# Sums of weights in HBM spread over the projections, with additions two behind their copies

## The chip, the cores and the metric

One core of a Trainium2 chip runs the kernel. The metric is device time in microseconds for one execution, lower being better. Times are medians over several executions, and profiles are of one execution each, which has its own time. A core has five engines that work side by side: TensorE (matmuls and transposes; PE in the profile), VectorE (DVE), ScalarE (ACT), GpSimd (POOL) and SyncE (SP, which here only issues transfers). Each goes through its own instructions in a fixed order, and waits on semaphores for the others. Transfers between HBM and the core's memory are issued by an engine into a queue, and 16 DMA engines carry them.

## The reference, cut to what matters

A decoder layer on 512 tokens of width 1024, all in float32:

```
h = rms_norm(x, norm_mix)
u, q, kc, vc, ks, vs, kw, vw, g_nsa, g_merge = split(h @ w_in)
y_pool = pool_mixer(u)                       # causal means over 2, 4, 8, 16 tokens, minus u, then w_pool
y_nsa  = nsa_mixer(q, ...)                   # 16 heads: compressed, selected and window attention, gated
g_a, g_b = split(sigmoid(g_merge))
x = x + (g_a * (y_pool @ w_proj_pool) + g_b * (y_nsa @ w_proj_nsa)) @ w_out
h = rms_norm(x, norm_mlp)
x = x + square(relu(h @ w_ff1)) @ w_ff2      # 1024 -> 4096 -> 1024
out = rms_norm(x, norm_final)
```

The compressed branch pools keys and values over 31 overlapping blocks of 32 tokens through a small MLP. At 512 tokens the selected branch takes all 8 blocks, so it and the window branch are causal attention, each over keys of its own.

## The kernel before, in words

**Arithmetic.** Each float32 operand is split into a high part of a shorter type (fp32r) and the remainder, its low part; a product is three matmuls: high by high, high by low, low by high (`mms`, L370). Activations stay on the chip. Weights come from HBM in pieces of 128 partitions by up to 1024 floats, 512 KB. ScalarE copies a piece into its high part (`wh`), and VectorE or POOL subtracts to get the low part (`wl`). For the projections, w_proj_nsa and w_out this goes by halves (L325 to L329): while attention and w_out run (`mode["pool"]`), VectorE makes the low part of the first half and POOL that of the second.

**Sums of weights.** Most of the MLP goes through seven block products in place of eight, in 14 groups (four column blocks of w_ff1 and three of w_ff2, two groups each). A group needs three sums of quarters of its weights, S1, S3 and S2, each 512 KB. They are formed in HBM long before the MLP loads them: a **copy**, which moves one quarter into the sum's place and is issued by SP (L256), then an **addition**, a DMA that adds a second quarter to what lies there and is issued by POOL (L252). S2 starts from a copy of the finished S1 (so its operands read S<-S in the profile). That makes 42 sums, in the list `jobs`: S1 and S3 of group 100, S1 and S3 of 101, S2 of 100, S1 and S3 of 200, S2 of 101 and so on (layer, block, group). Each addition waits on POOL for its copy to land, and each S<-S copy on SP for the addition of its S1. POOL computes nothing while it waits.

**Loads.** The list `LD` gives every piece of weights in order, 0 to 34 the projections of the first phase (`P1`: keys, values, compression MLP, pool branch, gates, first queries), 35 to 47 `FILL2` (queries q3 to q7 and gates gb0 to gb7), 48 to 55 w_proj_nsa (pn0 to pn7), 56 to 63 w_out (wo00 to wo13, half and row block), then from 64 (`MLP0`) the MLP. There are four raw buffers, so load i is issued when the piece i - 4 has been split. `emit_load` issues load i on SP (L223) and then calls `make_sum` as often as `sums_after(i)` says (L229 to L233). One call issues the addition of the sum before, on POOL, and the copy of the next sum, on SP; the compiler is told to keep the copy behind that load (`tc.issue_after`).

By `sums_after`, loads 0 to 36 start no sum, loads 37 to 51 start two each, then every second load to 62 starts one, and in the MLP every fourth.

**The stages, in the time of the profile.** Until about 44 us: norm and turning of the input. To 160: the projections of P1. Then FILL2, whose matmuls are there to fill TensorE beside the start of attention. Attention's first step (`cmp_scores`, L896 to L931): scores against compressed keys, a softmax on VectorE and ScalarE, the gate r (L916), and then on POOL the weighting `cw` (L918) and the split into `PC` (L920, L921). TensorE transposes PC into psT (L929), and nothing of the main loop is emitted ahead of that for the first pair of heads. The main loop runs over 96 slots (eight pairs of heads, query tiles, branches): scores (L959), maximum (L981), exponential (L991), weighting by the sum and the gate on POOL (L1004), transposes (L1020), their split (L1031 on ScalarE, L1035 on VectorE) and product with the values (L1045, L1054). It ends near 412. Then w_proj_nsa (pn), merging (L833), and w_out in two halves: the weights wo00 to wo03 are used as they come, four matmul groups of about 1.4 us each (psB L370), and wo10 to wo13 are split into a resident pair W1H, W1L, used once all four are there. The MLP starts near 480.

The order of the instructions is that in which the kernel's generator emits them: `ahead` (L344) puts a half of a weight's split between matmuls, a finished second half emits the next load, and the load emits its sums at that point. So a change of `sums_after` moves SP's copies and POOL's additions between other instructions.

Of the kernel before, what the change touches and what calls it, by code (L numbers as in the profile page):

```python
# [62 lines left out]
def trunk(ctx: ExitStack, tc: tile.TileContext, A, out):  # L63
# [41 lines left out]
    def add_key(k):  # L105
# [14 lines left out]
        else:  # L120
# [4 lines left out]
    P1 = ("ck ks u0 wk0 wk1 u1 wk2 u2 kw wk3 cv V0 V1 V2 wv0 u3 wv1 q0 wv2 wpool ga0 ga1 wv3 ga2 q1 "  # L125
          "ga3 ga4 ga5 q2 ga6 ga7 pp0 pp1 pp2 pp3").split()
    FILL2 = "gb0 q3 q4 q5 gb1 gb2 q6 gb3 q7 gb4 gb5 gb6 gb7".split()
# [7 lines left out]
    MLP0 = len(LD)  # L135
# [5 lines left out]
    jobs, late = [], []  # L141
# [62 lines left out]
    def emit_load():  # L204

        i = st["load"]
        if i >= len(LD):
            return False
        segs = LD[i]
        a = segs[0][0].shape[1]  # L210
        b = sum(s.shape[2] for s, _ in segs)
        assert a * b <= 1024
        if not by_name() or st["kept"] < RAW:
            st["kept"] += by_name()
            t = wp.tile([128, 1024], F32, tag="raw", bufs=RAW, name=f"raw{i}")
        elif spare:
            t = spare.pop(0)
        else:
            return False
        st["load"] += 1  # L220
        v = t[:, :a * b].rearrange("p (a b) -> p a b", a=a)
        for s, o in segs:
            began = nc.sync.dma_start(v[:, :, o:o + s.shape[2]], s)  # L223
        raws[i] = (t, a, b)
        for _ in range(sums_after(i)):
            make_sum(began)
        return True

    def sums_after(i):  # L229

        i -= len(P1) + 2
        n = len(FILL2) + 2
        return 2 if 0 <= i < n else i % 2 if n <= i < MLP0 - len(P1) - 2 else i % 4 == 0 and i > 0  # L233

    def by_name():

        return st["load"] >= MLP0

    def give_back(*tiles):
        spare.extend(tiles)  # L240
        while spare and by_name() and emit_load():
            pass

    def make_sum(load):

        n = st["sums"]
        if n > len(jobs):
            return
        st["sums"] += 1
        if n:  # L250
            to, _, q = jobs[n - 1]
            POOL.dma_start(to, q, accum_op=ALU.add)  # L252
        if n < len(jobs):
            to, q, _ = jobs[n]
            with tc.issue_after(load.ins):
                nc.sync.dma_start(to, q)  # L256
# [15 lines left out]
    def group_steps(i):  # L272

        key, at = WL[i]
        if isinstance(at, str):
            t = held.pop(key)
        else:
            while st["load"] <= at:
                assert emit_load()
            t = raws.pop(at)[0]  # L280
        h, l = slot_of(i)
        ACT.activation(h, t, AF.Copy)  # L282
        yield
        DVE.tensor_tensor(l, t, h.bitcast(F32), op=ALU.subtract)  # L284
        hls[i] = tuple(x.rearrange("p (a b) -> p a b", a=4) for x in (h, l))
        to = SUM_OF.get(key)
        if to is None:
            give_back(t)
        elif to not in held:
            held[to] = t  # L290
        else:
            yield
            DVE.tensor_tensor(t, t, held[to], op=ALU.add)
            give_back(held[to])
            held[to] = t

    def emit_prep_half():
# [12 lines left out]
        if "h" not in part:  # L310
            while st["load"] <= at:
                assert emit_load()
            if WL[i][0] in dest:
                h, l = dest[WL[i][0]][:2]
            else:
                h, l = slot_of(i)
            part.update(h=h, l=l, half=0)
# [295 lines left out]
    with ExitStack() as c1:  # L613
# [185 lines left out]
        for k in P1[2:]:  # L799
            i = int(k[-1]) if k[-1].isdigit() else None  # L800
# [35 lines left out]
    with ExitStack() as c2:  # L836
# [235 lines left out]
        n = len(slots)  # L1072
# [4 lines left out]
        for i in range(n + LAG + PLAG):  # L1077
            if i < n:
                p = slots[i][0]
# [480 lines left out]
```

## Time and profile before

| | |
|---|---|
| three runs | 841.06, 839.63, 840.54 us; median 840.54 |
| the profiled execution's own time | 837.06 us |
| its span in the profile | 835.1 us |
| mean granted clock of TensorE | 0.982 |

The profile has a page and views of the trace. In a row of instructions, L252 is line 252 of the kernel, `out<-in` are the names of its tiles, xN the number of instructions; in the view in order of time the first number is the start in us from the span's start, the second the length, and brackets hold the idle time of the engine just before and what ended it. In the table by windows each row gives the stretch, its length, the busy time of PE, PEld (weight loads into TensorE), DVE, ACT and POOL with their instructions, TensorE's granted clock as a share of full speed, the mean busy share of the 16 DMA engines (a little over 1 where the records overlap) and GB/s. A row of waits gives the engine, the tile and line that waited, what it waited for, total us, times, and the longest. In the table of DMA issues the last number is the median us from issue to landing. q1 is the queue of SP's transfers, q0 that of POOL's.

### The profile page before, as it was taken

The numbers are of one execution on the slowest core, as the hardware profiler recorded it, in microseconds if no ns is written. First come the engines' busy times: TensorE is split into PE (matmuls) and PEld (weight loads), VectorE is DVE, ScalarE is ACT, GpSimd is POOL, SyncE is SP. The second block draws the span as 40 slices with busy tenths as digits, with TensorE's granted clock in tenths as the row PEclk, the third lists the DMA queues.
The fourth block names the chain that finished last, engine by engine and source line by source line (L and its number), as shares of the span: only waits on it lengthen the run. The fifth ranks groups of instructions, "written<-read, shape, count | busy, mean of one in ns | idle before, by whom it ended". The sixth has DMA issues, their size and how long they took to land.

```text
span 835.1 us, 13944 instructions
## 1 busy us (share of the span) xinstructions
PE 792.6 (95%) x5081; PEld 708.6 (85%) x5081; DVE 614.2 (74%) x1195; ACT 483.8 (58%) x959; POOL 214.1 (26%) x277
## 2 busy tenths in 40 slices
PE   7999999983899899999999999999999999999997
PEld 4889878872787788888788789999999999999986
DVE  7796744531897998989766569897789678987823
ACT  6576533332686888789823457664575467446811
POOL 6000000024877797876233400100000000000000
PEclk9999999995899999999999999999999999999999
DMA  9364633599809988577397932968543644365402
GB/s 301 99 181 116 170 89 106 152 255 252 165 15 240 227 164 165 127 181 148 132 248 178 301 74 79 265 191 249 172 143 113 216 147 170 105 200 177 151 1 101
DMA packets 125502, 137.15 MB, mean 164 GB/s; under 512 B 5365, under 2 KB 112409, under 8 KB 125210
## 3 DMA queue, kind: packets, MB, share of 16 engines
q1 hardware_dynamic: 102970, 113.46, 42.6%
q0 software_dynamic: 22176, 22.02, 17.9%
q8 instruction: 40, 0.66, 0.3%
q10 hardware_dynamic: 288, 0.79, 0.3%
q14 instruction: 28, 0.23, 0.1%
HBM read 131.53 MB, written 46.14 MB: 213 GB/s over the span
## 4 chain that ended last, share of the span: by engine, by line
PE 63%; DVE 16%; DMA 7%; ACT 6%; issue 4%; POOL 2%; SPq 1%; ACTq 0%; POOLq 0%; DVEq 0%
PE psF L370 16%; PE psB L1329 13%; PE psB L370 12%; PE psB L1445 9%; DMA S<-w_ff 4%; PE psO L1054 2%; PE psT L1020 2%; PE psS L959 2%; DVE wl L284 2%; PE psV L370 2%; DVE PT L1035 1%; DVE P L981 1%; ACT P L991 1%; PE psF L424 1%; DMA raw<-w_out 1%
## 5 line engine op out<-in xcount | busy, mean ns | idle before, releaser
L370 PE MATMUL psF<-R,wh 128*128 128x512 f32 x512 | 166.8, 404 | 0.2 <-ACT MA L817 0.2
L282 ACT ACTIVATE wh<-raw 128x1024 fp32r<-128x1024 f32 x66 | 69.7, 1057 | 78.2 <-PE psB L1445 30.7
L327 ACT ACTIVATE wh<-raw 128x512 fp32r<-128x512 f32 (+1 forms) x102 | 61.3, 620 | 84.5 <-PE psF L370 35.8
L370 PEld LDWEIGHTS psF<-R,wh 128*128 128x128 f32 x512 | 92.6, 189 | 18.0 <-ACT MA L817 0.5
L1004 POOL TENSOR_SCALAR P<-P,sm,GT 128x128 f32<-128x128 f32 (+3 forms) x128 | 98.1, 979 | 21.5 <-DVE sm L1001 14.7
L370 PE MATMUL psF<-R,wl 128*128 128x512 f32 x256 | 101.8, 398 | 0.7 <-DVE wl L329 0.7
L252 POOL DMA_DIRECT2D S<-w_ff x42 | 53.9, 1283 | 177.9 <-DMA S<-w_ff 117.7
L284 DVE TENSOR_TENSOR wl<-raw,wh 128x1024 fp32r<-128x1024 f32 x66 | 80.4, 1220 | 22.3 <-ACT wh L282 22.1
L329 DVE TENSOR_TENSOR wl<-raw,wh 128x512 fp32r<-128x512 f32 (+1 forms) x78 | 56.1, 731 | 38.0 <-ACT wh L327 37.6
L991 ACT ACTIVATE P<-P,sm 128x128 f32<-128x128 f32 (+3 forms) x128 | 71.1, 557 | 18.2 <-DVE sm L981 16.7
L981 DVE CUSTOM_DVE_ANT_0 P<-psS,cst 128x128 f32<-128x128 f32 (+3 forms) x128 | 59.6, 483 | 23.6 <-PE psS L959 16.0
L1329 PE MATMUL psB<-R,wh 128*128 128x256 f32 x352 | 64.1, 282 | 0.0
L1525 POOL TENSOR_TENSOR MA<-x,GB 128x512 f32<-128x512 f32 x1 | 1.3, 1292 | 238.8 <-DVE sq L1205 238.8
L1031 ACT ACTIVATE PT<-psT 128x512 fp32r<-128x512 f32 (+2 forms) x96 | 49.2, 521 | 18.3 <-PE psT L1020 17.5
L1035 DVE TENSOR_TENSOR PT<-psT,PT 128x512 fp32r<-128x512 f32 (+2 forms) x96 | 56.6, 593 | 4.4 <-ACT PT L1031 3.5
L370 PEld LDWEIGHTS psF<-R,wl 128*128 128x128 f32 x256 | 48.3, 189 | 11.8 <-DVE wl L329 0.9
L282 ACT ACTIVATE w3h<-raw 128x1024 fp32r<-128x1024 f32 x32 | 33.8, 1057 | 39.6 <-PE psB L1445 14.8
L1020 PE MATMUL psT<-ident,P 128*128 128x128 f32 x320 | 52.1, 279 | 4.0 <-POOL P L1004 3.6
L1329 PEld LDWEIGHTS psB<-R,wh 128*128 128x128 f32 x352 | 54.1, 189 | 0.3 <-DVE R L1271 0.2
L1020 PEld LDWEIGHTS psT<-ident,P 128*128 128x128 f32 x320 | 40.4, 143 | 15.1 <-POOL P L1004 6.5
L329 POOL TENSOR_TENSOR wl<-raw,wh 128x512 fp32r<-128x512 f32 x28 | 41.5, 1483 | 37.0 <-ACT wh L327 37.0
L1329 PE MATMUL psB<-R,wl 128*128 128x256 f32 x176 | 49.4, 281 | 0.0
(431 smaller groups left out, 2319.1 us busy)
## 6 DMA issues: line engine op xcount, KB each, us to landing
raw<-w_ff SPq DMA_DIRECT2D x50, 512.0 KB, 4.1
S<-w_ff POOLq DMA_DIRECT2D x42, 512.0 KB, 7.5
raw<-S SPq DMA_DIRECT2D x42, 512.0 KB, 4.1
raw<-w_in SPq DMA_DIRECT2D x32, 512.0 KB, 4.1
S<-w_ff SPq DMA_DIRECT2D x28, 512.0 KB, 6.3
S<-S SPq DMA_DIRECT2D x14, 512.0 KB, 7.2
raw<-w_proj_nsa SPq DMA_DIRECT2D x8, 512.0 KB, 4.0
raw<-w_out SPq DMA_DIRECT2D x8, 512.0 KB, 5.1
```

The source lines that it names most:

```text
L282: ACT.activation(h, t, AF.Copy)
L284: DVE.tensor_tensor(l, t, h.bitcast(F32), op=ALU.subtract)
L327: ACT.activation(h[:, sl], t[:, sl], AF.Copy)
L329: eng.tensor_tensor(l[:, sl], t[:, sl], h[:, sl].bitcast(F32), op=ALU.subtract)
L370: PE.matmul(ps, a, b, start=first and j == 0, stop=last and j == n - 1, skip_group_check=True)
L981: DVE.tensor_tensor_reduce(out=P[:, o:o + n].rearrange("p (a c) -> p a c", c=128), in0=s, in1=m, scale=1.0, scalar=3e38, op0=ALU.add, op1= ...
L991: last_exp[:] = [ACT.activation(c, c, AF.Exp, bias=sm[:, 0, e:e + 1], scale=-1.0, accum_out=sm[:, 1, e:e + 1])]
L1004: POOL.tensor_scalar(P[:, o:o + n], P[:, o:o + n], sm[:, 2, e:e + 1], GT[:, qb, c + e:c + e + 1], op0=ALU.mult, op1=ALU.mult)
L1020: PE.transpose(pt[:, 128 * j:128 * j + 128], P[:, 128 * j:128 * j + 128], ident)
L1035: DVE.tensor_tensor(dL, src, dH.bitcast(F32), op=ALU.subtract)
L1329: PE.matmul(out, w[u][:, k, 128 * f:128 * f + 128], XB[x][v][:, k, :], **kw)
L1445: PE.matmul(out, YB[y][u][:, k, 128 * f:128 * f + 128], w[v][:, k, :], **kw)
```

## The change

Two things. `sums_after` is rewritten: of the P1 loads, 11, 13, ... 29 start one sum each (ten), loads 30 to 36 none, loads 37 to 51 one each instead of two, loads 52 to 63 in turn one, two and none, and in the MLP every fourth load, as before, but from load 64 where it was 65. And `make_sum` issues the addition of the sum two before, not of the one before, so that another copy lies between a copy and its addition.

```diff
@@ -222,15 +222,18 @@
         for s, o in segs:
             began = nc.sync.dma_start(v[:, :, o:o + s.shape[2]], s)
         raws[i] = (t, a, b)
-        for _ in range(sums_after(i)):
+        for _ in range(int(sums_after(i))):
             make_sum(began)
         return True
 
     def sums_after(i):
 
-        i -= len(P1) + 2
-        n = len(FILL2) + 2
-        return 2 if 0 <= i < n else i % 2 if n <= i < MLP0 - len(P1) - 2 else i % 4 == 0 and i > 0
+        p, f = len(P1), len(P1) + len(FILL2)
+        if i < p:
+            return 10 <= i < 30 and i % 2
+        if i < MLP0:
+            return p + 2 <= i < f + 4 or i >= f and i % 3
+        return i % 4 == 0
 
     def by_name():
 
@@ -244,11 +247,11 @@
     def make_sum(load):
 
         n = st["sums"]
-        if n > len(jobs):
+        if n > len(jobs) + 1:
             return
         st["sums"] += 1
-        if n:
-            to, _, q = jobs[n - 1]
+        if n > 1:
+            to, _, q = jobs[n - 2]
             POOL.dma_start(to, q, accum_op=ALU.add)
         if n < len(jobs):
             to, q, _ = jobs[n]
```

The lines behind are numbered three higher in the changed kernel.

## The prediction, made before the changed kernel ran

> **What bounds the kernel now.** I read the totals and the DMA queues, then the waits of TensorE, then busy time by window where TensorE falls short.
>
> ```profile
> PE 792.6 (95%) x5081; PEld 708.6 (85%) x5081; DVE 614.2 (74%) x1195; ACT 483.8 (58%) x959; POOL 214.1 (26%) x277
> ...
> q1 hardware_dynamic: 102970, 113.46, 42.6%
> q0 software_dynamic: 22176, 22.02, 17.9%
> ```
> ```profile
> PE psT L929 <- POOL PC L921: 14.7, 1, 14.7
> ```
> ```profile
> 80.00:100.00 20.00, 20.00 (x96) 16.43 (x95) 14.01 (x28) 8.96 (x17) 0.00 (x0) 1.00 0.75 199
> ...
> 180.00:200.00 20.00, 5.34 (x24) 3.99 (x22) 1.39 (x2) 2.25 (x5) 7.62 (x8) 0.69 1.14 247
> 200.00:220.00 20.00, 16.20 (x69) 13.53 (x69) 13.71 (x42) 10.11 (x31) 12.12 (x18) 0.71 1.04 249
> ...
> 460.00:480.00 20.00, 19.88 (x86) 15.81 (x85) 11.10 (x11) 8.55 (x15) 8.68 (x7) 1.00 0.98 304
> ```
> TensorE is busy for 95% of the span, so time can only come from where it is not. One wait of 14.7 us, behind POOL's PC at L921, is a third of all its idle time. It lies in 180 to 200, where TensorE works 5.34 of 20 us, its granted clock falls to 0.69, and the DMA engines are full (share 1.14, the last column but one). One addition costs 17.9% of 835.1 us over 42, 3.56 us of all 16 engines; a copy or a load of 512 KB costs q1's 42.6% over 113.46 MB, 1.64 us. Windows 80 and 460 are the stages that receive work: TensorE is full in both, the DMA at 0.75 and 0.98.
>
> The wait in POOL's and the other engines' order of time:
>
> ```profile
> 165.48 2.57 POOL L252 DMA_DIRECT2D S<-w_ff  x2 [35.12 <-DMA S<-w_ff]
> ...
> 174.27 1.36 POOL L329 TENSOR_TENSOR wl<-raw,wh 128x512 fp32r<-128x512 f32 x1 [0.61 <-ACT wh L327]
> ...
> 194.47 1.16 POOL L252 DMA_DIRECT2D S<-w_ff  x1 [5.11 <-DMA S<-w_ff]
> 195.11 1.15 POOL L918 TENSOR_TENSOR cw<-cw,c 128x256 f32<-128x256 f32 x1
> 195.85 1.55 POOL L252 DMA_DIRECT2D S<-w_ff  x1
> ...
> 197.76 1.30 POOL L920 TENSOR_SCALAR PC<-cw 128x256 fp32r<-128x256 f32 x1
> 199.14 0.72 POOL L921 TENSOR_TENSOR PC<-cw,PC 128x256 fp32r<-128x256 f32 x1
> ...
> 207.40 1.17 POOL L252 DMA_DIRECT2D S<-w_ff  x1 [4.22 <-DMA S<-w_ff]
> 208.15 2.15 POOL L1004 TENSOR_SCALAR P<-P,sm,GT 128x128 f32<-128x128 f32 x4
> ```
> ```profile
> 179.72 0.17 DVE L916 TENSOR_TENSOR c<-c,GT 128x8 f32<-128x8 f32 x1
> ```
> ```profile
> 199.92 0.75 PE L929 MATMUL psT<-identR,PC 128*128 128x128 f32 x4 [14.66 <-POOL PC L921]
> ...
> 209.12 0.89 PE L1020 MATMUL psT<-ident,P 128*128 128x128 f32 x2 [2.30 <-POOL P L1004]
> ```
> L918 could start when L916 is done at 179.9, but POOL goes in order and seven additions stand ahead of it, an eighth behind it, each waiting for its copy to land. TensorE is out of work at 199.92 - 14.66 = 185.26. A second wait follows at once: the softmax weights stand behind one more addition (207.40).
>
> **The change, part by part.** No arithmetic is added or removed: 42 copies and 42 additions stay, at other places. The built order puts ten additions before POOL's VC copies of L724 and four, not seven, ahead of L918, none between L918 and L921.
>
> ```profile
> raw<-w_in SPq DMA_DIRECT2D x4, 512.0 KB, 3.7
> ...
> S<-w_ff SPq DMA_DIRECT2D x2, 512.0 KB, 5.9
> ```
> ```profile
> S<-w_ff SPq DMA_DIRECT2D x5, 512.0 KB, 6.9
> S<-w_ff POOLq DMA_DIRECT2D x4, 512.0 KB, 12.1
> raw<-w_in SPq DMA_DIRECT2D x3, 512.0 KB, 12.9
> S<-S SPq DMA_DIRECT2D x1, 512.0 KB, 9.5
> ```
> ```profile
> 175.77 0.66 SPq L223 DMA_DIRECT2D raw<-w_in  x1
> ...
> 198.71 0.37 SPq L223 DMA_DIRECT2D raw<-w_in  x1
> 199.14 2.07 SPq L256 DMA_DIRECT2D S<-w_ff  x2
> ```
> These are issues with their median time to landing, first from 120 to 160 us, then from 160 to 180, then SP's order.
>
> *Ten sums moved into the projections* (from about 44 to 120 us): 10 x (3.56 + 1.64) = 52 us of DMA over some 75 us, beside a load of 0.75 in the window shown. Loads there may go from 3.7 towards 12.9 us. POOL is idle there (0.00), so the additions hold no engine; two behind, they find their copies landed. TensorE is covered by four raw buffers. I take 0; if the cover is gone, a load 9.2 us late costs at most that once.
>
> *The wait at L921.* The last of the four additions before L918 is that of S2 of group 201. Its copy (S<-S) is issued behind the load of gb2, 175.77 + 0.4 = 176.2. It lands 4.7 us later when alone (row below) and 9.5 us later among four additions; two are in flight now, so I take 7.4: 183.6. POOL then needs 0.2 to see it, 0.64 (195.11 - 194.47), and 0.74 + 1.38 + 0.78 from L918 to L929 without the pieces between: 3.7. L929 starts at 187.3, 12.6 earlier; the bounds are 14.66 (TensorE ready first) and 10.5.
>
> *The second wait stays.* After L921 come a low half (1.3 us), the load of q6 that it frees, the copy 0.43 behind (199.14 - 198.71) and its addition, still ahead of the first weights: 187.3 + 1.3 + 0.1 + 0.43 = 189.1, landing 5.9 to 8.3 later (207.40 - 199.14); I take 6.3, then 0.75: weights at 196.1, not 208.15. So 12.0 us are gained there, not 12.6: TensorE waits longer at L1020, and the low clock after it (0.71) stays.
>
> *Attention.* Fourteen additions leave POOL's line: 14 x 1.16 = 16 us of an engine off the path.
>
> ```profile
> 215.00:412.00 197.00, 188.49 (x1202) 163.48 (x1201) 170.91 (x546) 163.94 (x430) 143.59 (x191) 1.00 0.69 151
> ```
> TensorE is idle 8.5 us there; that bounds the gain, 0 the other way. I take 1.
>
> *The stage of w_out pays.* Loads 52 to 63, pn4 to wo13, start twelve sums, not six: 6 x 5.2 = 31 us of DMA more where it was near full. Three additions now stand ahead of the low half of pn6, two ahead of that of wo01.
>
> ```profile
> raw<-w_out SPq DMA_DIRECT2D x5, 512.0 KB, 5.6
> ...
> S<-S SPq DMA_DIRECT2D x1, 512.0 KB, 4.7
> ```
> ```profile
> 426.03 0.56 SPq L256 DMA_DIRECT2D S<-w_ff  x1
> ```
> ```profile
> 432.79 1.16 POOL L252 DMA_DIRECT2D S<-w_ff  x1 [1.62 <-DMA S<-w_ff]
> 435.44 1.33 POOL L329 TENSOR_TENSOR wl<-raw,wh 128x512 fp32r<-128x512 f32 x1 [1.49 <-ACT wh L327]
> ...
> 446.64 1.33 POOL L329 TENSOR_TENSOR wl<-raw,wh 128x512 fp32r<-128x512 f32 x1 [2.51 <-ACT wh L327]
> ...
> 454.31 1.80 POOL L329 TENSOR_TENSOR wl<-raw,wh 128x512 fp32r<-128x512 f32 x1
> ```
> ```profile
> 451.84 0.63 ACT L327 ACTIVATE W1H<-raw 128x512 fp32r<-128x512 f32 x1 [2.65 <-DMA raw<-w_out]
> 452.38 1.14 ACT L327 ACTIVATE wh<-raw 128x512 fp32r<-128x512 f32 x2
> ```
> ```profile
> 456.54 0.40 PE L370 MATMUL psB<-wh,mH 128*128 128x512 f32 x1
> ```
> In times of before: the third copy is issued at 427.4 and lands 6.9 to 12.9 later, I take 439; pn6's low half moves from 435.44 to 439.9, and the load that it frees with it. TensorE does not wait: it needs that half at 442.5 (two weights of 5.6 us before 450.94, less half of one). The next copy lands near 449, so wo00's low half runs at 449.8, not 446.64, and wo10's load is issued 3 us late, at 451.1. It lands 8 us later (between 5.6 and 12.9, two copies ahead of it), at 459.1, not 451.8. ScalarE takes wo10 first and wo01 (452.38) behind it, and wo01 is due at 456.54 with some 2.4 us to spare: TensorE waits 7.3 - 2.4 = 4.9. The new order also puts half of wo11 ahead of wo02 on ScalarE; wo11's load starts when wo01's low half is done, lands 5.6 later and needs 2 us of conversion, against 5.6 us of matmuls: 2 more. Together 7; the bounds are 0 (loads stay within the 2.4) and 16 (all at 12.9).
>
> The rows say 3.7 against 12.9 us for a load beside additions, though they are on another queue. The Trainium skill, DMA: Bandwidth & Descriptors, section on queues, rings and completion order, says that an engine takes turns between queues packet by packet. By that a w_out load, in 256 rows of 2 KB, lets fewer pieces of an addition pass than a w_in load in 1024 rows of 512 B; the second rival is what that would give.
>
> **Sum.** 0 - 12 - 1 + 7 = -6 us. The profiled execution's own time is 837.06 us (span 835.1): 831.1. The runs' median, 840.54, is 3.5 above it: 834.5.
>
> **Rivals.**
> Second, *the w_out loads hold*: they land in 5.6 us, as five of them do above, only 2 us later than alone, within the 2.4 to spare. Then -12 - 1 + 1 = -12, and 828.5. For it: w_out's rows are large, and the copies alone take 5.9. Against: wo10's load starts late whatever it takes.
> Third, *the w_out stage takes all back*, at wo01. If the third copy takes 12.9 us, pn6's low half and each load behind it starts 6 us late, and wo10's load lands 18 late in all (6 + 12.9 - 3.8 + 3): less 2.4, and 2 at wo02, 17.6 us against 13. That gives 845, slower. It decides from wo10 landing 13 us late. For it: 460 to 480 is at 0.98 before six more sums. Against: the largest delays stand beside four additions at once.
> Fourth, *the change misses its wait*: gb2's load and the copy behind it are as slow as now (12.9), L929 at 193, a gain of 7, all given back: 840.5.
>
> **Chances.** The forecast 0.44, the second 0.26, the third 0.17, the fourth 0.13. About 0.2% (1.7 us) can be told from no change. Faster: 0.44 + 0.26 + 0.03 of the fourth; same: 0.08 of it; slower: the third and 0.02. The forecast's own range is 830 to 838.5; with the second down to 826 and the third up to 843, less than 2 in 10 is left out.
>
> **What would show it.** Right: the wait at L929 under 4 us, one at L1020 of 4 to 6, weights near 196; new waits of TensorE for wl at the second and third w_out weights, ScalarE waiting for DMA raw<-w_out before W1H; the DMA share near 1 from 420 to 480. The forecast is wrong if POOL still waits for S ahead of L918 after 185 us, if TensorE waits in 44 to 160, or if no wait stands between 440 and 475.

## The result, and the profile after

The changed kernel is slower by 0.6%: median 845.41 us over 19 runs (840.73 to 852.67) against 841.06 us (836.76 to 843.86) for the kernel before, a ratio of 1.006 with a 95% interval of 1.0037 to 1.0082. The forecast was 834.5 in a range of 826 to 843. The profiled execution took 847.01 us, 10 us more than the one of before (837.06).

The page of the changed kernel, first the totals, then its waits of TensorE (total us, times, longest), then those from 60 to 120 us alone:

```profile
span 845.2 us, 13936 instructions
...
PE 797.1 (94%) x5081; PEld 709.0 (84%) x5081; DVE 607.9 (72%) x1195; ACT 483.3 (57%) x959; POOL 213.0 (25%) x277
```
```profile
PE psT L1023 <- POOL P L1007: 5.3, 3, 4.0
PE psB L373 <- ACT wh L330: 4.9, 1, 4.9
```
```profile
PE psF L373 <- DVE yd L792: 2.4, 1, 2.4
PE psF L373 <- ACT MA L820: 2.2, 1, 2.2
PE psV L373 <- DVE wl L332: 1.9, 2, 1.4
PE psV L373 <- ACT wh L330: 0.8, 1, 0.8
```

The wait of 14.7 us at psT is gone: of the 5.3 us left there, 4.0 are the second wait that the prediction kept. In place of the long one stand many small ones in stages that had none. The busy time by window shows where, first for the kernel before, then for the changed one (columns as in the table of the prediction; the last but one is the DMA share):

```profile
44.00:80.00 36.00, 36.00 (x207) 32.00 (x206) 30.94 (x66) 25.16 (x52) 0.00 (x0) 1.00 0.48 130
...
100.00:120.00 20.00, 19.80 (x89) 15.77 (x88) 8.41 (x15) 7.56 (x15) 0.00 (x0) 1.00 0.30 85
...
412.00:480.00 68.00, 66.21 (x284) 52.87 (x283) 43.54 (x46) 24.92 (x43) 25.83 (x20) 1.00 0.86 240
```
```profile
44.00:80.00 36.00, 33.32 (x188) 29.12 (x187) 27.65 (x58) 22.52 (x44) 4.79 (x4) 1.00 1.00 250
...
100.00:120.00 20.00, 15.34 (x58) 11.81 (x57) 11.32 (x23) 7.68 (x15) 2.31 (x2) 0.84 1.15 269
...
180.00:200.00 20.00, 19.61 (x94) 15.93 (x93) 7.62 (x15) 6.88 (x12) 7.36 (x8) 1.00 1.07 239
...
412.00:480.00 68.00, 56.70 (x229) 43.54 (x229) 35.57 (x36) 19.81 (x35) 29.01 (x24) 0.95 1.08 274
```

From 180 to 200 us TensorE now works 19.61 of 20 us (5.34 before). The first transposes of PC and of P in its order of time:

```profile
199.31 0.36 PE L932 MATMUL psT<-identR,PC 128*128 128x128 f32 x2 [0.39 <-POOL PC L924]
...
208.66 0.33 PE L1023 MATMUL psT<-ident,P 128*128 128x128 f32 x1 [4.04 <-POOL P L1007]
```

The first waits 0.39 us, the second 4.04. From 44 to 120 and from 412 to 480 us it falls behind, and there the DMA share has gone to about 1 or above.

The account by stages goes by the time at which a stage's first or last matmul starts in the trace: the projections from the first psV (L373) to the first product of yd with w_proj_pool; FILL2 from there to the first transpose of PC (L932); attention to the last psO (L1057); then w_proj_nsa; the w_out stage from wo00's first matmul to the last transpose of xs (L1258); the MLP to its last matmul. The first four columns are the stages that change, in us; the sums in loads 42 to 51 and in loads 52 to 63 stand in the last two columns.

| kernel | projections | FILL2, wait | attention | w_out | median, us | 42-51 | 52-63 |
|---|---|---|---|---|---|---|---|
| before | 90.1 | 48.7 | 209.1 | 52.3 | 841.06 | 20 | 6 |
| changed | 103.3 | 34.4 | 206.3 | 67.3 | 845.41 | 10 | 12 |
| tail_before | 97.0 | 34.7 | 209.3 | 54.1 | 834.49 | 15 | 6 |
| no_sums_p1 | 90.1 | 34.8 | 212.3 | 67.4 | 843.94 | 20 | 12 |
| late_p1_tail_before | 90.1 | 37.5 | 212.7 | 54.1 | 828.80 | 20 | 6 |
| lag_two_only | 90.1 | 47.9 | 210.5 | 54.1 | 837.94 | 20 | 6 |
| p1_adds_out | 90.1 | 34.7 | 206.2 | 65.4 | 837.45 | 10 | 12 |
| p1_ten_late | 90.1 | 35.3 | 206.6 | 66.1 | 836.64 | 10 | 12 |
| wo_low_dve | 100.6 | 34.5 | 206.0 | 64.1 | 843.38 | 10 | 12 |
| sums_in_mlp | 90.1 | 33.9 | 200.2 | 53.1 | 814.82 | 15 | 1 |
| wo_adds_out | 100.4 | 35.9 | 209.2 | 54.9 | 832.88 | 10 | 12 |
| one_behind | 99.4 | 34.7 | 207.7 | 71.0 | 847.96 | 10 | 12 |
| ten_late_mlp | 90.1 | 34.0 | 201.2 | 52.4 | 813.83 | 10 | 3 |
| rope_on_act | 99.4 | 34.7 | 215.2 | 65.0 | 851.65 | 10 | 12 |

For the two kernels of the case: projections +13.2, FILL2 with its wait -14.3, attention -2.8, w_out +15.0, and 1 less in the rest: +10, the difference of the two profiled executions. The projections' loss is not the same in each execution: five further kernels have the changed kernel's spread up to load 36, and their profiles show 97.0 to 100.6 (one with additions one behind, one with other rope transfers). The profile of the changed kernel is the worst of them, which is part of why the medians are only 4.4 us apart.

**The loss in the projections.** The changed kernel's trace, ScalarE, VectorE and TensorE in order of time (start, length; idle before and what ended it in brackets), and the DMA issues from 50 to 72 us, of before and then of the changed kernel:

```profile
62.26 1.15 ACT L330 ACTIVATE wkt<-raw 128x512 fp32r<-128x512 f32 x2 [4.67 <-DMA raw<-w_cv]
...
65.10 0.44 ACT L330 ACTIVATE wh<-raw 128x304 fp32r<-128x304 f32 x1
...
66.91 0.46 DVE L332 TENSOR_TENSOR wl<-raw,wh 128x304 fp32r<-128x304 f32 x1
...
67.42 0.41 PE L373 MATMUL psV<-wl,R 128*128 128x304 f32 x1 [0.45 <-DVE wl L332]
...
70.61 0.41 PE L373 MATMUL psV<-wl,R 128*128 128x304 f32 x1 [1.43 <-DVE wl L332]
```
```profile
raw<-w_cv SPq DMA_DIRECT2D x3, 512.0 KB, 3.9
...
rs<-rx SPq DMA_DIRECT2D x4, 64.0 KB, 2.0
```
```profile
raw<-w_cv SPq DMA_DIRECT2D x2, 512.0 KB, 9.3
...
rs<-rx SPq DMA_DIRECT2D x4, 64.0 KB, 5.9
```

The load that is late is that of wv0 (issued at 52.90, landed 9.3 us later, with an addition in flight from 50.59 to 60.5), which TensorE does not need yet. But ScalarE splits it (wkt, 62.26) ahead of the second weight of V, whose load had long landed, and so that half (65.10, low part 66.91) reaches TensorE late. Four raw buffers cover a late load for the weight in it, not for what is queued behind its conversion. The second place is the rope of q1:

```profile
108.13 0.76 DVE L574 TENSOR_TENSOR rx<-rx,cst 128x256 f32<-128x256 f32 x2 [5.96 <-DMA rs<-rx]
...
110.88 0.97 PE L373 MATMUL psF<-yd,wpl 128*128 128x512 f32 x3 [2.44 <-DVE yd L792]
...
114.66 1.22 PE L373 MATMUL psF<-R,wh 128*128 128x512 f32 x2 [2.22 <-ACT MA L820]
115.68 0.63 PE L373 MATMUL psF<-R,wl 128*128 128x512 f32 x1
...
120.66 0.40 PE L373 MATMUL psF<-R,wl 128*128 128x512 f32 x1
```

VectorE stands 5.96 us at the rope's exchange transfers, and yd and the weights behind it are late for TensorE. After the two waits a matmul takes 0.63 us instead of 0.40 for 6 us, until 120.66, at a granted clock of 0.52: here the waits cost more than their length. How the loss divides between the two places no run separates.

**The loss in the w_out stage**, in the changed kernel's order of time:

```profile
447.41 1.17 POOL L255 DMA_DIRECT2D S<-w_ff  x1 [8.15 <-PE psB L373]
448.07 1.79 POOL L332 TENSOR_TENSOR wl<-raw,wh 128x512 fp32r<-128x512 f32 x1
```
```profile
438.52 0.49 SPq L259 DMA_DIRECT2D S<-S  x1
...
449.89 0.37 SPq L223 DMA_DIRECT2D raw<-w_out  x1
```
```profile
458.57 0.63 ACT L330 ACTIVATE W1H<-raw 128x512 fp32r<-128x512 f32 x1 [13.93 <-DMA raw<-w_out]
459.11 0.61 ACT L330 ACTIVATE wh<-raw 128x512 fp32r<-128x512 f32 x1
```
```profile
449.91 0.50 PE L373 MATMUL psB<-wl,mH 128*128 128x512 f32 x1 [1.33 <-POOL wl L332]
459.77 0.80 PE L373 MATMUL psB<-wh,mH 128*128 128x512 f32 x1 [4.93 <-ACT wh L330]
462.24 0.79 PE L373 MATMUL psB<-wl,mH 128*128 128x512 f32 x1 [1.67 <-DVE wl L332]
471.79 0.50 PE L373 MATMUL psB<-wl,mH 128*128 128x512 f32 x1 [1.28 <-POOL wl L332]
497.43 0.33 PE L1258 MATMUL psB<-ident,xs 128*128 128x128 f32 x1 [2.01 <-DVE xs L1216]
```

POOL stands at the addition of 447.41 until the copy before it, issued at 438.52, has landed after 8.3 us at 446.84 (the bracket names TensorE, but its work had been done before). Only then does it make the low half of wo00 (448.07), whose buffer wo10's load needs. So that load is issued at 449.89, and it lands 8.7 us later (ScalarE takes it at 458.57). wo01, which TensorE needs first, stands behind it on ScalarE (459.11). TensorE waits 4.93 us there and 1.3 to 2.0 us at four more places.

### The profile page after: what moved, and what is told of

Same layout as the page of the kernel before. It is cut to its first block, busy times and chain, and to the rows that moved or that the text cites. A ratio compares the mean times of both kernels' runs of the same rounds, so it can differ in the third digit from the quotient of the medians.

```text
span 845.2 us, 13936 instructions
## 1 busy us (share of the span) xinstructions
PE 797.1 (94%) x5081; PEld 709.0 (84%) x5081; DVE 607.9 (72%) x1195; ACT 483.3 (57%) x959; POOL 213.0 (25%) x277
## 4 chain that ended last, share of the span: by engine, by line
PE 62%; DVE 17%; DMA 7%; ACT 7%; issue 3%; POOL 3%; SPq 0%; DVEq 0%; ACTq 0%; POOLq 0%
PE psF L373 16%; PE psB L1332 15%; PE psB L373 10%; PE psB L1448 9%; PE psO L1057 3%; PE psT L1023 2%; PE psS L962 2%; DMA raw<-w_out 2%; DVE P L984 2%; PE psF L427 2%; DVE PT L1038 1%; DMA raw<-w_ff 1%; DVE wl L287 1%; ACT P L994 1%; DMA raw<-w_cv 1%
## 5 line engine op out<-in xcount | busy, mean ns | idle before, releaser
L373 PE MATMUL psF<-R,wh 128*128 128x512 f32 x512 | 168.3, 407 | 2.4 <-ACT MA L820 2.4
L255 POOL DMA_DIRECT2D S<-w_ff x42 | 49.6, 1207 | 259.5 <-DMA S<-w_ff 155.5
L373 PEld LDWEIGHTS psF<-R,wh 128*128 128x128 f32 x512 | 93.7, 191 | 20.7 <-ACT MA L820 3.0
L330 ACT ACTIVATE wh<-raw 128x512 fp32r<-128x512 f32 (+1 forms) x102 | 61.1, 619 | 83.0 <-PE psF L373 34.5
L373 PE MATMUL psF<-R,wl 128*128 128x512 f32 x256 | 102.5, 401 | 0.8 <-DVE wl L332 0.8
L1007 POOL TENSOR_SCALAR P<-P,sm,GT 128x128 f32<-128x128 f32 (+3 forms) x128 | 88.4, 758 | 32.3 <-DVE sm L1004 21.9
L332 DVE TENSOR_TENSOR wl<-raw,wh 128x512 fp32r<-128x512 f32 (+1 forms) x78 | 60.6, 788 | 42.6 <-ACT wh L330 42.2
L1332 PE MATMUL psB<-R,wh 128*128 128x256 f32 x352 | 64.1, 282 | 0.0
L1023 PE MATMUL psT<-ident,P 128*128 128x128 f32 x320 | 51.5, 275 | 8.1 <-POOL P L1007 5.3
L373 PEld LDWEIGHTS psF<-R,wl 128*128 128x128 f32 x256 | 48.8, 191 | 12.1 <-DVE wl L332 0.9
L1023 PEld LDWEIGHTS psT<-ident,P 128*128 128x128 f32 x320 | 39.8, 140 | 19.2 <-POOL P L1007 11.2
L287 DVE TENSOR_TENSOR w3l<-raw,w3h 128x1024 fp32r<-128x1024 f32 x32 | 39.1, 1222 | 14.7 <-ACT w3h L285 14.6
```

Source lines behind the costliest of these rows:

```text
L330: ACT.activation(h[:, sl], t[:, sl], AF.Copy)
L332: eng.tensor_tensor(l[:, sl], t[:, sl], h[:, sl].bitcast(F32), op=ALU.subtract)
L373: PE.matmul(ps, a, b, start=first and j == 0, stop=last and j == n - 1, skip_group_check=True)
L1007: POOL.tensor_scalar(P[:, o:o + n], P[:, o:o + n], sm[:, 2, e:e + 1], GT[:, qb, c + e:c + e + 1], op0=ALU.mult, op1=ALU.mult)
L1023: PE.transpose(pt[:, 128 * j:128 * j + 128], P[:, 128 * j:128 * j + 128], ident)
L1332: PE.matmul(out, w[u][:, k, 128 * f:128 * f + 128], XB[x][v][:, k, :], **kw)
```

## The experiments

Each is an edit of the changed kernel. The medians of before beside them were 840.74 (first four), 841.65 (next four) and 840.63 us (last four).

**tail_before**: the w_out stage alone goes back to before's spread, and attention takes five sums more.

```diff
-        if i < MLP0:
-            return p + 2 <= i < f + 4 or i >= f and i % 3
-        return i % 4 == 0
+        if i < p + 7:
+            return i >= p + 2
+        if i < f + 4:
+            return 1 + i % 2
+        return i % 2 == 0 if i < MLP0 else i % 4 == 1
```

> Ten sums in the projections as in the changed kernel, one at each of loads 37 to 41, 15 in loads 42 to 51, and from load 52 on the spread of before (every second load, then every fourth). Theory A (three separate terms, each paid or gained in its own stage: projections +13.7 us in the profile, the wait at psT -14.3, the w_out stage +15 between the first matmul of wo00 and the last transpose of xs): the w_out stage goes back to before's 52 us and the rest stays, so about 845.4 - 13 = 832 (827 to 837), with the projections still late by 9 to 14 us. Rival B (the w_out stage is slow because copies and additions of the new order, two behind, collide there, not because there are six more of them): 840 or more, the stage still over 60 us.

Measured: 834.49 us (828.47 to 838.33), ratio 0.9916 [0.9891, 0.9942]. The w_out stage took 54.1 us, the projections 97.0. Theory A holds for the w_out stage: six sums more in it cost 13 us. The projections lost 6.9 us here, less than the 9 to 14 expected.

**no_sums_p1**: no sum in the projections, ten more in attention.

```diff
-        if i < p:
-            return 10 <= i < 30 and i % 2
-        if i < MLP0:
-            return p + 2 <= i < f + 4 or i >= f and i % 3
-        return i % 4 == 0
+        if i < p + 7:
+            return i >= p + 2
+        if i < f + 4:
+            return 2
+        return i % 3 if i < MLP0 else i % 4 == 0
```

> No sum in the projections; one at each of loads 37 to 41, two at each of loads 42 to 51; from load 52 on as in the changed kernel, additions two behind. Theory A: the projections lose nothing (TensorE not idle from 44 to 160), the wait at psT stays under 3 us as there are still only a few additions ahead, the w_out stage pays its 15: 845.4 - 13 = 832 (827 to 837). Rival C (the delay of the projections costs nothing by itself, since TensorE would have had to wait at psT for the same additions anyway): the wait at psT comes back by what the projections gain, 843 to 847. Rival D (ten more sums within attention hold POOL and the DMA engines there): attention longer by 5 or more, 837 to 842.

Measured: 843.94 us (839.77 to 848.0), ratio 1.0035 [1.0008, 1.0061]. The total is that of rival C, but the trace isn't: the waits of TensorE from 60 to 215 us were

```profile
PE psT L1023 <- POOL P L1007: 5.1, 2, 4.8
...
PE psT L932 <- POOL PC L924: 0.8, 1, 0.8
```

so the projections gained their 13 us (90.1) and psT waits only 0.8. What came instead is an attention of 212.3 us instead of 206.3, which is rival D; the median lies 4 us above the profiled 839.77, and no stage here tells why. So theory A was incomplete: sums can have a price in attention too. Its size is not settled: the kernel before, with as many sums there, took 209.1. The ten sums ahead of load 37 were not needed to remove the wait at psT; fewer at loads 37 to 41 were enough.

**late_p1_tail_before**: five late sums in the projections, and before's spread from load 52 on.

```diff
-            return 10 <= i < 30 and i % 2
+            return i >= 26 and i % 2 == 0
-        if i < MLP0:
-            return p + 2 <= i < f + 4 or i >= f and i % 3
-        return i % 4 == 0
+        if i < p + 7:
+            return i >= p + 2
+        if i < f + 4:
+            return 2
+        return i % 2 == 0 if i < MLP0 else i % 4 == 1
```

> Five sums in the projections, late ones (loads 26, 28, 30, 32, 34), one at each of loads 37 to 41, two at each of 42 to 51, from load 52 on as in before, additions two behind. Theory A: projections +0 to 2 (the loads there have a matmul group of 5.6 us each and the DMA engines were at 0.3 to 0.35), psT -14, attention 0 to -3, w_out stage 0: 841 - 14 = 827 (822 to 831), faster than both kernels. Rival D (as above, attention pays): 830 to 836. Rival B: 838 or more.

Measured: 828.80 us (826.67 to 831.78), ratio 0.9858 [0.982, 0.9897], faster than both kernels. Projections 90.1, w_out 54.1, attention 212.7: theory A but for attention, which is again over 212.

**lag_two_only**: before's `sums_after` with the changed kernel's `make_sum`.

```diff
-        p, f = len(P1), len(P1) + len(FILL2)
-        if i < p:
-            return 10 <= i < 30 and i % 2
-        if i < MLP0:
-            return p + 2 <= i < f + 4 or i >= f and i % 3
-        return i % 4 == 0
+        i -= len(P1) + 2
+        n = len(FILL2) + 2
+        return 2 if 0 <= i < n else i % 2 if n <= i < MLP0 - len(P1) - 2 else i % 4 == 0 and i > 0
```

> The spread of before, with additions two behind their copies instead of one: the second half of the change alone. Theory A: seven additions stay ahead of L918 less one, copies unchanged; the wait at psT goes from 14.7 to 10 to 14: 838 to 841. Rival E (the second half alone removes the wait, because each addition finds its copy landed): the wait under 4 us, 828 to 831. Rival B: the w_out stage over 60 us, 848 or more.

Measured: 837.94 us (835.91 to 847.12), ratio 0.9986 [0.9957, 1.0014]: no difference that can be told. Its trace has the wait at psT at 13.87 us and a w_out stage of 54.1, 1.8 us longer than before's, as in the two other kernels that have before's spread there and additions two behind. Rival E falls.

**p1_adds_out**: without the first eight of the ten additions that run during the projections (eight sums stay unfinished).

```diff
-        if n > 1:
+        if n > 9:
             to, _, q = jobs[n - 2]
             POOL.dma_start(to, q, accum_op=ALU.add)
```

> The changed kernel without the eight additions that POOL issues during the projections (the first eight sums stay unfinished, so the output is another one); all copies stay. Theory A1 (the additions are what delays the projections: a load beside one lands in 9 to 10 us, one beside copies alone in 5 to 6): the projections, from the first psV to the first matmul of pp0, take 90 to 92 us as in before, not 97 to 103; the whole about 845 - 8 = 837 (833 to 841). Rival A2 (the ten copies on SP's own queue, ahead of the loads, delay them): the stage still 96 or more, the whole 842 or more.

Measured: 837.45 us (832.17 to 843.04), ratio 0.995 [0.9918, 0.9981], projections 90.1. With the ten copies and the last two additions (at 105.80 and 118.79) nothing is lost: A1. It was the additions. From 62 to 103.3 us the DMA share is 0.78 here, with copies and no addition, against 0.99 in the changed kernel; whether an addition hurts as such or by the traffic that it adds, no run separates.

**p1_ten_late**: ten sums as in the changed kernel, at other loads.

```diff
-            return 10 <= i < 30 and i % 2
+            return i >= 25
```

> The changed kernel with its ten P1 sums at loads 25 to 34, one each, not at every second load from 11 to 29. Theory A3 (what costs is the place: the bursts of loads around V0 to wv1 and around ga0 to q1, and not the ten sums): the projections as in before, 90 to 92 us; the whole 845 - 8 = 837 (833 to 841). Rival A4 (ten sums cost there in any place, as the DMA engines fall behind: 6.8 us of transfers for each 6.2 us of matmuls): a stage of 95 or more, or the wait at psT back at over 6 us, the whole 842 or more.

Measured: 836.64 us (835.39 to 838.09), ratio 0.9947 [0.9925, 0.9969], projections 90.1, psT waits 1.1 us. The row of windows of this kernel from 93 to 144 us, where its sums lie, and that of the changed kernel from 62 to 103.3:

```profile
93.00:144.00 51.00, 50.79 (x223) 40.46 (x223) 25.08 (x52) 19.41 (x36) 11.07 (x12) 1.00 1.08 258
```
```profile
62.00:103.30 41.30, 37.45 (x210) 32.21 (x209) 27.57 (x57) 23.41 (x49) 4.60 (x4) 1.00 0.99 230
```

The DMA engines are as full in the one as in the other (1.08 and 0.99), and TensorE loses 0.2 us in the one and 3.9 in the other. The rest of the changed kernel's loss lies behind 103.3. From load 25 on, each load has a matmul group of 5.6 us to hide under; from V0 to q1 loads come in bursts, two or three within 2 us, and the rope's transfers stand between. A3 holds: the place cost, not the number. Nor need a late rope cost anything: in this kernel VectorE waits for it up to 5.8 us, and TensorE's only wait from 60 to 170 us is one of 0.2.

**wo_low_dve**: VectorE makes the second low halves after attention, so that none stands behind an addition on POOL.

```diff
+    mode["pool"] = False
     p3 = ctx.enter_context(pool("p3"))
```

> The changed kernel with the second low halves of w_proj_nsa (from pn2 on) and w_out made by VectorE, not POOL, so that none stands behind an addition. Theory W1 (the order on POOL: low halves behind additions free the raw buffers late, and the loads are issued late): the w_out stage, from the first matmul of wo00 to the last transpose of xs, falls from 67.3 to 55 to 60; the whole 836 to 840. Rival W2 (the DMA engines are full with six sums more, whoever makes the halves): the stage stays at 63 or more, the whole 842 or more.

Measured: 843.38 us (840.66 to 846.63), ratio 1.0016 [0.9985, 1.0048], w_out stage 64.1. The waits of TensorE and of ScalarE from 440 to 500 us:

```profile
PE psB L1259 <- DVE xs L1217: 5.0, 1, 5.0
PE psB L373 <- DVE wl L332: 1.3, 2, 0.9
PE psB L373 <- ACT wh L330: 1.1, 2, 0.8
```
```profile
ACT W1H L330 <- DMA raw<-w_out: 18.9, 4, 8.8
...
ACT w3h L285 <- DMA raw<-w_ff: 5.7, 1, 5.7
```

The wait at wo01 is gone (the longest for wh is 0.8, not 4.9), so the order on POOL was its nearest cause. But the loads still land late, and the loss moves on: ScalarE stands 5.7 us at the MLP's first loads, ahead of the squares that xs needs, and TensorE waits 5.0 us for xs. Of 15 us only 3 come back: W2; from 444 to 470 us the DMA share is 1.15.

**sums_in_mlp**: few sums early, none with pn5 to wo13, and 18 in the MLP.

```diff
-            return 10 <= i < 30 and i % 2
-        if i < MLP0:
-            return p + 2 <= i < f + 4 or i >= f and i % 3
-        return i % 4 == 0
+            return i >= 26 and i % 2 == 0
+        if i < p + 7:
+            return p + 2 <= i < p + 5
+        if i < f + 4:
+            return 1 + i % 2
+        return i % 4 == 0 and (i == f + 4 or i >= MLP0)
```

> Fewer sums early and more in the MLP: five in the projections (loads 26 to 34, every second), three at loads 37 to 39, 15 at loads 42 to 51, one at 52, none with pn5 to wo13, and one behind every fourth load of the MLP until all 42 are made (18 there instead of 6). Theory A (each sum costs where the DMA engines or POOL are near their limit; in the MLP, at 0.49 of the DMA engines, it costs nothing): projections 0, psT wait under 3.5, attention 3 us shorter than with 20 sums, w_out stage 52: 828.8 - 5 = 824 (820 to 828). Rival M (the additions slow the MLP's loads, TensorE waits for wh there): 830 or more, with waits after 510 us.

Measured: 814.82 us (813.02 to 817.26), ratio 0.9692 [0.9648, 0.9737], the fastest of all that compute the whole. Its page and windows:

```profile
PE 787.9 (97%) x5081; PEld 704.9 (87%) x5081; DVE 604.4 (75%) x1195; ACT 482.7 (60%) x959; POOL 215.1 (27%) x277
```
```profile
160.00:215.00 55.00, 52.30 (x291) 43.91 (x290) 36.15 (x116) 32.26 (x87) 29.26 (x40) 1.00 0.62 144
...
400.00:480.00 80.00, 79.52 (x373) 64.78 (x372) 46.68 (x64) 34.07 (x67) 18.88 (x14) 1.00 0.41 118
480.00:800.00 320.00, 318.24 (x2503) 309.44 (x2502) 256.44 (x318) 182.05 (x259) 19.81 (x17) 1.00 0.70 198
```

In the MLP the DMA share is 0.70 and TensorE works 318.24 of 320 us: 18 sums cost nothing there. Rival M falls. It beat its own expectation by 9 us. Some 5 of them lie at the first softmax weights: with no sum at loads 40 and 41 no addition stands ahead of them, and from the first transpose of PC to the first of P it takes 4.8 us, against 9.2 before and 9.4 in the changed kernel. The other 4 are not accounted for.

**wo_adds_out**: without the eleven additions that loads 53 to 62 start (eleven sums stay unfinished).

```diff
-        if n > 1:
+        if n > 1 and not 25 < n < 37:
             to, _, q = jobs[n - 2]
             POOL.dma_start(to, q, accum_op=ALU.add)
```

> The changed kernel without the eleven additions that loads 53 to 62 start (eleven sums stay unfinished, so the output is another one); the copies stay, and so do the loads. Theory W2 (the additions fill the DMA engines, and loads and copies beside them take 7 to 16 us): the w_out stage, from the first matmul of wo00 to the last transpose of xs, falls from 67.3 to 52 to 55; the whole 845 - 13 = 832 (828 to 836). Rival W3 (the copies on SP's queue, between the loads, are what delays them): the stage stays over 60, the whole 838 or more.

Measured: 832.88 us (830.68 to 836.03), ratio 0.9908 [0.9877, 0.9939], w_out stage 54.9: W2 again. With the twelve copies the stage is still 2.5 us longer than in the kernel before (54.9 against 52.3), which has six copies and six additions there; sums_in_mlp, with one sum, took 53.1, so the twelve copies cost some 2 us and the eleven additions 12.4.

**one_behind**: the changed kernel's `sums_after` with before's `make_sum`.

```diff
-        if n > len(jobs) + 1:
+        if n > len(jobs):
             return
         st["sums"] += 1
-        if n > 1:
-            to, _, q = jobs[n - 2]
+        if n:
+            to, _, q = jobs[n - 1]
```

> The changed kernel's spread with additions one behind their copies, as in before: the first half of the change alone. Theory A (where the sums lie decides, not how far the additions are behind): 845 (841 to 849), the w_out stage 63 to 70, the wait at psT under 4. Rival E (additions two behind were needed: one behind, POOL stands waiting for each copy ahead of L918 and ahead of the low halves): psT waits over 6 us, the whole 850 or more.

Measured: 847.96 us (843.63 to 854.81), ratio 1.0093 [1.0059, 1.0127], w_out stage 71.0. PC's transposes wait 0.7 us at psT and P's 5.0. Theory A but for 1 us in the stage: one behind, the stage is 3.7 us longer, by one profile of each; the other effects are the spread's.

**ten_late_mlp**: ten sums at loads 25 to 34, none to load 41, one each at 42 to 54, the rest in the MLP.

```diff
-            return 10 <= i < 30 and i % 2
+            return i >= 25
         if i < MLP0:
-            return p + 2 <= i < f + 4 or i >= f and i % 3
+            return p + 7 <= i < f + 7
```

> Ten sums at loads 25 to 34, none from 35 to 41 (so that no addition stands ahead of L918 or the first weights), one at each of loads 42 to 54, and from load 64 one behind every fourth load until 42 are made; additions two behind. Theory A: projections 0, no wait at psT nor at the first transposes, attention 2 us shorter than with 16 sums there, w_out stage 52 to 53, MLP as in sums_in_mlp: 814.8 - 3 = 812 (809 to 816). Rival A4 (ten late sums fill the DMA engines from 100 to 170 us, and the additions left over hold POOL ahead of L918): a wait at psT over 3 us, 816 or more.

Measured: 813.83 us (813.09 to 815.51), ratio 0.9684 [0.9659, 0.9709], the same as sums_in_mlp within their ranges. But it computes something else at one place: S2 of group 130 is loaded as load 139, and its addition comes only with load 140, so that group works with a sum that lacks its second quarter. One sum more before the MLP, as in sums_in_mlp, is needed to be in time.

**rope_on_act**: the rope's exchange transfers issued by ScalarE.

```diff
-            nc.sync.dma_start(sw[32 * b:32 * b + 32, :], xr[32 * a:32 * a + 32, :])
+            nc.scalar.dma_start(sw[32 * b:32 * b + 32, :], xr[32 * a:32 * a + 32, :])
```

> The changed kernel with the four exchange transfers of each rope (rs from rx) issued by ScalarE on a queue of its own instead of by SP behind loads and copies. Theory R1 (in the projections the largest piece of the loss comes through the rope of q1: its transfers land after 6 to 9 us, VectorE waits 6 us for them in order, and the halves and yd behind it are late): the projections, first psV to first matmul of pp0, 93 to 96 us instead of 97 to 103; the whole 839 to 842. Rival R2 (the additions slow every queue alike, or the loads alone are late enough): the stage still 97 or more, the whole 843 or more.

Measured: 851.65 us (849.24 to 856.65), ratio 1.0145 [1.01, 1.0191]. The projections took 99.4 us, within what they vary, and attention 215.2, 9 more, with ScalarE issuing all ten ropes' transfers. The DMA issues from 60 to 120 us:

```profile
S<-w_ff POOLq DMA_DIRECT2D x8, 512.0 KB, 8.6
...
rs<-rx ACTq DMA_DIRECT2D x4, 64.0 KB, 5.7
```

On a queue of their own they still land after 5.7 us (5.9 on SP's from 50 to 72 us, 2.0 there without sums): it is not the order on SP's queue that makes them late. So the edit did not make the rope's transfers early, and what the rope of q1 costs by itself stays open; R1's forecast of 93 to 96 us failed.

## Why the prediction was wrong, point by point

- *The ten sums in the projections, "I take 0; if the cover is gone, a load 9.2 us late costs at most that once"*: this is the step that failed. Loads did slow to 9 to 10 us from issue to landing, within the 12.9 that it allowed, but the four raw buffers covered only the weight in the late load, not the halves that ScalarE and VectorE convert behind it, nor what VectorE makes behind a late rope. Nor was the price paid once: it was +13.2 us in the profile and 6.9 to 10.5 in five others. Moving the same sums to loads 25 to 34 or leaving out eight of their additions takes it to 0. The stage was priced by its mean DMA share; its bursts, two or three loads within 2 us, were not looked at. The prediction's own sign of being wrong, TensorE waiting in 44 to 160, came.
- *The wait at L921*: right. Forecast 12.6 us earlier; the wait is gone but for 0.4, so its upper bound of 14.66 was reached. In the changed kernel TensorE also came 13 us later to this point, but that is not what removed the wait: p1_ten_late, whose projections lose nothing, waits 1.1 and transposes PC at 187.48, where the forecast had 187.3. The fourth rival (the change misses its wait) fell.
- *The second wait stays*, 4 to 6 us: 4.04 at L1023, behind one addition on POOL. Right; the clock after it was less low than forecast (0.91 from 200 to 220 us, 0.71 before). sums_in_mlp shows what this stretch was worth: about 5 us, which the prediction left standing.
- *Attention, -1*: -2.8 in this profile; other profiles of the same spread in attention show 206.0 to 209.2, so its size isn't settled better than that.
- *The stage of w_out, +7 (0 to 16)*: the mechanism was right, the term half of what was measured. wo10's load was forecast 3 us late and 8 us under way: it came 5.4 late (449.89 against 448.0 - 3.46, the stage having begun 3.46 us earlier) and took 8.7; the wait at wo01 was forecast 4.9 and measured 4.93. That the two agree so closely is luck: the load landed 10.2 us late, not 7.3, but wo01's high half had more than the 2.4 to spare (in the kernel before it was done 3.5 us ahead of its matmul), and TensorE itself came 1.8 us later to wo01. wo02, forecast at 2, waited 1.28 for its low half. Missing were the waits for the low halves of wo00 (1.33) and wo01 (1.67) and for xs (2.01), and the slow clock behind wo01 (0.50 from 459.7 to 463; 0.80 us instead of 0.40 for the matmul at 459.77). The whole came to 15.0, inside the bound of 16.
- *The third rival* (the w_out stage takes all back, 845): its total is what was measured, by luck. It had 17.6 us there, with wo10 landing 13 us late or more, and nothing in the projections; measured were 15.0, with wo10 10.2 late, and +13.2 in the projections.
- *The second rival* (w_out's large rows hold their own against additions): fell. w_out's loads landed 5.3 to 9.9 us after issue, 8.7 in the median from 438 to 462. The Trainium skill, DMA: Bandwidth & Descriptors, section on queues, rings and completion order, says that an engine takes turns packet by packet. No run here shows the turns themselves; the conclusion drawn from them, that large rows would be slowed little, was wrong.
- *That additions two behind find their copies landed*: wrong. POOL's waits over the whole of the changed kernel:

```profile
POOL S L255 <- DMA S<-w_ff: 155.5, 17, 49.8
POOL S L255 <- DMA S<-S: 80.1, 9, 34.2
```

So POOL stood waiting for a copy at 26 of its 42 additions (by the same view at 17 in the kernel before). "Two behind" holds for the order in which the program emits them. But in the projections POOL has nothing else to do: it comes to each addition before the copy has landed, and issues it 0.3 us after the landing in most cases. So the second half of the change was worth nothing measurable by itself (lag_two_only, 0.9986 [0.9957, 1.0014]).

In sum: of the gain at psT 12 were forecast, and 14.3 came; +13.2 where 0 was forecast and +15.0 where 7 was gave it back twice, in the two profiles. The medians are closer together, +4.4, where -6 was forecast.

## What to carry to other kernels

Work that only needs to be done in time belongs where its own deadline puts it, in a stage that has DMA time free; here 18 of 42 sums could wait for the MLP, which needs them last and had half its DMA time free. That, with five sums at late loads of the projections and none just ahead of the first softmax weights, gave 3.1%, where moving sums to an earlier engine that stood idle gave a loss. To price background transfers in a stage, take not its mean DMA share but the tightest burst of loads in it and what is queued in order behind a late one. One wait of 14.7 us on a page is easier to see than ten of 1 to 5 us, but removing it by traffic elsewhere can cost as much.

## What the runs showed of the hardware that was not expected

- An addition in HBM issued by POOL weighs on its neighbours far more than a copy of the same 512 KB: the twelve copies of the w_out stage cost some 2 us there and the eleven additions 12.4; in the projections ten copies with two additions cost nothing, and the other eight additions 7 to 13 us. An addition also takes more of the engines, 3.56 us against 1.64 by the rows of the prediction; that this is the whole reason is not shown.
- A 64 KB transfer beside additions takes 5.7 to 5.9 us on either queue, against 2.0 without sums: 4 us more, where a 512 KB load of w_cv takes 5 more (9.3 against 3.9).
- DMA engines at a share of 1.08 for 51 us cost TensorE 0.2 us where every load had 5.6 us of matmuls ahead of it.
- After waits of 2.44 and 2.22 us TensorE ran at 0.63 us a matmul instead of 0.40 for 6 us, at a granted clock of 0.52 (114.66 to 120.66). The Trainium skill, TensorE: Matmul & The Clock Gate, part 1, says that the clock halves after an idle window of some 3.4 us and returns after a busy one; here two waits shorter than that, with some 1.5 us of matmuls between, were enough.
